# Token and weight sums of a two-level fast product moved and recut in a hybrid decoder step

## The chip, the cores and the metric

The kernel runs on one core of one Trainium2 chip. The core has TensorE (PE, matmuls; PEld is its weight load), VectorE (DVE), ScalarE (ACT), GpSimd (POOL) and SyncE (SP), which here issues nearly all DMAs. The metric is the device time of one execution in microseconds (us). Less is better.

## The reference

One step of a single-layer decoder for a prompt of 1024 tokens and 8 sample tokens (1032 columns in all), model width 2048. Everything is in float32.

```python
p = project(rmsnorm(x, norm_w), w_in)       # one product, 2048 x 7768, split by columns
att = dsa(p)        # indexer scores, top 256 keys, softmax attention, 8 heads x 128
h_ml = mlstm(p)     # 4 heads, chunked gated recurrence, states C, n, m
a  = att * silu(p['az'])
hn = h_ml * rsqrt(mean(h_ml ** 2) + 1e-6) * ml_norm_w
mo = hn * sigmoid(p['mo']) * silu(p['mz'])
y  = rmsnorm(x + concat([a, mo]) @ w_out, final_norm_w)
# also returned: k, v, indexer keys and the mLSTM states, of prompt and samples
```

The kernel keeps float32 accuracy by splitting each operand into a high part H (rounded for TensorE) and a low part L = x - H, and by adding three matmuls: HH, HL and LH.

## The kernel before, in words

**The projection.** The weights' columns are cut into 61 tiles of 128. Tile 0 is misc (indexer key, gates), tiles 1 to 8 the indexer's queries (iq), 9 to 16 the mLSTM values (computed by `vproj` with weights and tokens in both roles), 17 to 36 attention k, v, q and mLSTM q, k (`T_AK` = 17, `T_AQ` = 21, `T_MQ` = 29, `T_G` = 37), and 37 to 60 the 24 gate tiles. `proj` computes tiles 0 to 8 and 17 to 36 in four quarters each: a quarter loads 256 KB of weights, casts them (ACT makes H, DVE makes L) and multiplies. The tokens stay in SBUF, split, as `xH[k]` and `xL[k]`, k from 0 to 15. `evac` multiplies results by the row factors and writes them out through DMAs.

**The gate tiles** are computed in pairs by a seven-product scheme of the Strassen kind: tokens are cut into two halves of `HR` = 516 columns, k into two halves of 8, output columns into the two tiles of a pair (`NP` = 12 pairs). It needs four weight sums for each pair (`job_usum`, in DRAM as `usD`) and five token sums for each k of 8 (`job_prep`, in DRAM as `xsD`), both made beforehand, beside the projection. Then `gate_stage` runs 7 x 12 products of 48 matmuls of 258 columns (`CS`), `product`, each in two quarters q of the k range and two column pieces c. Products 4 and 6 (plain weights) come first, then 1, 3, 2 and at last 0 and 7. Partial results go out to `spD` (`put`) and come back (`get`); `combine` adds PSUM to them; `gate_mo`, `gate_mz` and `gate_az` apply tanh, the products with earlier results, and write `gateS`. `fill` brings token sums from `xsD` into the slots of `xH`, `xL` that are no longer wanted; the upper columns of `xH[8..15]`, `xL[8..15]` serve as buffers for split weights, and the `rstd` tile, the rings `wst` and `evp` lend spill buffers (`outs`).

**Jobs beside the main line.** Three lanes of generators are stepped after each quarter of a tile. A job has a start tile, an end tile and a weight, and is paced so that it ends at its end tile: lane 0 has the chunk gates, the indexer (`job_index`, DVE and ACT loops that find the top 256), the prompt's attention (`job_att`) and mLSTM (`job_ml`); lane 1 the token sums (`prep`, tiles 4 to 17), then the sample tokens' work (`dscore`, `dsel`, `datt`, `dml`); lane 2 the weight sums (`usum`, tiles 4 to 31). Their matmuls are ordered on PE between those of the tiles. The tool that builds the program orders each engine's instructions by its own timeline; what `pin` marks stays behind everything written before it on its engine.

`job_prep` works in 32 steps of one k and a quarter of the columns (`cw` = 129): two loads of `X`, three multiplications on DVE, four sums on POOL, one cast (L1375) and one subtraction (L1376) of all five sums, and two DMAs (L1378) to `xsD` with runs of 129 numbers. `sH` and `sL` have one buffer each. `job_usum` does, for each pair and each of four sums, a copy DRAM to DRAM issued by SP (L1387) and an accumulating DMA issued by POOL (L1389).

**PSUM.** Eight banks: three `pj` for the main products, five in the ring `bank()` for everything else. The gate stage takes a fourth for itself out of the ring for its whole length, so that two products alternate between two pairs of banks; the jobs have four.

After the gate stage, the output product `w_out` is computed, first for the last 264 columns, then for 768 columns by a seven-product scheme again, with the final norm.

Of the kernel before, what the change touches and what calls it, by code (L numbers as in the profile page):

```python
# [59 lines left out]
NX = 4  # L60
# [42 lines left out]
class Job:  # L103
    def __init__(self, name, start, end, weight, gen, *conds):
        self.name, self.start, self.end, self.weight, self.gen, self.conds = name, start, end, weight, gen, conds

# [43 lines left out]
def body(tc, A, stop=None):  # L150
# [8 lines left out]
    wst = ctx.enter_context(tc.tile_pool(name="wst", bufs=3))  # L159
# [52 lines left out]
    spD = dt_([3, NP, 2, 128, CS], "spD")  # L212
# [29 lines left out]
    evp = evctx.enter_context(tc.tile_pool(name="evp", bufs=6))  # L242
    xctx = ExitStack()
    xp = xctx.enter_context(tc.tile_pool(name="xp", bufs=1))
    xH = [xp.tile([128, R], F32R, name=f"xH{k}") for k in range(KT)]
    xL = [xp.tile([128, R], F32R, name=f"xL{k}") for k in range(KT)]
# [297 lines left out]
    def job_att():  # L544
# [4 lines left out]
        with tc.tile_pool(name="at", bufs=2) as pa:  # L549
# [65 lines left out]
            def soft(pair, S2):  # L615
                g, i, hp = pair
                cs = cuts((i + 1) * 128)
                for hh in range(2):
                    st = S2["st"][hh]
                    if len(cs) == 2:  # L620
                        V.tensor_tensor(st[:, 0:1], st[:, 0:1], st[:, 1:2], OP.max)
                    V.tensor_scalar(st[:, 2:3], st[:, 0:1], -ATT_SCALE, None, OP.mult)
# [4 lines left out]
                    if len(cs) == 2:  # L627
                        V.tensor_tensor(st[:, 3:4], st[:, 3:4], st[:, 4:5], OP.add)

            def start():  # L630
                return {"st": [pa.tile([128, 6], F32, name="st", bufs=4) for _ in range(2)], "P": [[], []]}
# [44 lines left out]
            for n, pair in enumerate(pairs):  # L676
# [21 lines left out]
                for hh in range(2):  # L698
                    V.reciprocal(cur["rc"][:, hp * 2 + hh, i:i + 1], now["st"][hh][:, 3:4])
# [82 lines left out]
    def job_ml():  # L782
        gT = mlc["gT"]
        with tc.tile_pool(name="ml", bufs=2) as pm:
# [72 lines left out]
            def main(c, h0, dk, dv, kv):  # L857
# [29 lines left out]
                for hh in range(2):  # L887
                    hms.append(pm.tile([128, 256], F32, name="hm"))
                    V.tensor_scalar(hms[hh], nds[hh][:, :256], st[:, 5, hh:hh + 1], None, OP.mult)
# [455 lines left out]
    def job_prep():  # L1345
        cw = CS // 2
        with tc.tile_pool(name="sx", bufs=1, side="right") as px:
            halves = rstd.rearrange("p (h t) -> p h t", h=2)
            steps = [(k, c) for k in range(8) for c in range(0, HR, cw)]

            def load(k, c):
                X = px.tile([128, 4, cw], F32, name="X", bufs=2)
                for y in range(2):
                    pin(SY.dma_start(X[:, 2 * y:2 * y + 2],
                                     A["xT"][k + 8 * y].rearrange("p (h t) -> p h t", h=2)[:, :, c:c + cw]))
                return X

            nxt = load(*steps[0])
            yield 1
            for n, (k, c) in enumerate(steps):  # L1360
                X = nxt
                if n + 1 < len(steps):
                    nxt = load(*steps[n + 1])
                O = px.tile([128, 5, cw], F32, name="O")
                lo, hi = nw[:, k:k + 1], nw[:, k + 8:k + 9]
                pin(V.scalar_tensor_tensor(X[:, 0:2], X[:, 0:2], lo, halves[:, :, c:c + cw], OP.mult, OP.mult))
                V.scalar_tensor_tensor(O[:, 0], X[:, 3], hi, halves[:, 1, c:c + cw], OP.mult, OP.mult)
                V.scalar_tensor_tensor(X[:, 2], X[:, 2], hi, halves[:, 0, c:c + cw], OP.mult, OP.mult)
                G.tensor_tensor(O[:, 1], X[:, 1], O[:, 0], OP.subtract)
                G.tensor_tensor(O[:, 2], O[:, 1], X[:, 0], OP.subtract)  # L1370
                G.tensor_tensor(O[:, 3], X[:, 0], X[:, 1], OP.subtract)
                G.tensor_tensor(O[:, 4], X[:, 2], O[:, 2], OP.add)
                yield 1
                H, L = (px.tile([128, 5, cw], F32R, name="s" + y) for y in "HL")
                pin(SC.copy(H, O))  # L1375
                V.tensor_tensor(L, O, H.bitcast(F32), OP.subtract)  # L1376
                for y, x in enumerate((H, L)):
                    SY.dma_start(xsD[:, k, y, :, c:c + cw].rearrange("o p t -> p o t"), x.bitcast(F32))  # L1378
                yield 1

# [20 lines left out]
    def ix_weight(blocks):  # L1401
# [10 lines left out]
             Lane([Job("prep", 4, T_AK, 65, job_prep),  # L1412
# [4 lines left out]
             Lane([Job("usum", 4, T_MQ + 2, 8 * NP, job_usum)])]  # L1417
# [189 lines left out]
    def gate_stage():  # L1607
        nonlocal pb0
        spare = [[x[8 + k][:, HR:HR + 512].rearrange("p (a b) -> p a b", a=4) for k in range(8)] for x in (xH, xL)]
        Hs, Ls = spare  # L1610
        free = [wst.tile([128, 4, 128], F32, name="w" + y, bufs=b)
                for y, b in (("raw", 2), ("H", 3), ("L", 3)) for _ in range(b)]
        raws, outs = free[:NX], [w.rearrange("p a b -> p (a b)") for w in free[NX:]]
        outs += [evp.tile([128, CN], F32, name="ev") for _ in range(6)]
        outs = [e[:, :CS] for e in outs]
        turn = {"raw": 0, "w": 0, "ev": 0}
        pj = [psj.tile([128, 512], F32, name=f"pj{x}") for x in range(3)] + [bank()]
        pj = [p[:, :CS] for p in pj]
# [630 lines left out]
```

## Time and profile before

| | us |
|---|---|
| median of 3 runs | 2232.45 (2230.85 to 2240.81) |
| the profiled execution | 2224.26 |
| its span, first to last instruction | 2222.5 |
| PE busy | 1982.8 |
| DVE, ACT, POOL busy | 1439.8, 943.1, 449.4 |
| mean granted TensorE clock | 0.95 |
| DMA | 440.96 MB in 340364 packets, mean 198 GB/s |

Busy time counts instructions that compute, not waits. A wait is listed as "who waited <- who ended the wait", with its total, count and longest. L and a number is a line of the kernel. A group's row has its count, busy us and mean ns, then the idle time of the engine just before its instructions and what ended it. Matmuls overlap in the pipeline, so their mean durations are longer than the time from one to the next.

### The profile page before, as it was taken

Reading aid. Unit: us, or ns where it says so; the run is one execution under the profiler, and the core shown is the slowest. Engines: PE = TensorE matmul, PEld = TensorE weight load, DVE = VectorE, ACT = ScalarE, POOL = GpSimd, SP = SyncE. Lnnn points to the kernel's source line nnn. Section 1 sums busy time; section 2 is a strip of 40 time slices with the busy share of each in tenths; the row PEclk is TensorE's granted clock in tenths of the full one; section 3 lists DMA queues with packets and bytes.
Section 4 is the critical chain, followed back from the end, with each engine's and each line's share of the span. In section 5 each row is a group of like instructions: output and inputs, shape, how many; then the busy total and the mean of one; then the engine's idle time right before and its main releaser. Section 6 shows DMA issues by size and latency. Waiting matters only on the chain. (4 is left out here: it accounts for less than half of the span.)

```text
span 2222.5 us, 37235 instructions
## 1 busy us (share of the span) xinstructions
PE 1982.8 (89%) x12710; PEld 1861.7 (84%) x12710; DVE 1439.8 (65%) x3451; ACT 943.1 (42%) x2025; POOL 449.4 (20%) x580
## 2 busy tenths in 40 slices
PE   9957368787899999999999999999988884999997
PEld 9956257676799999999999999999988884987886
DVE  8322325555566876869685555655577884789787
ACT  7111123343235323453133445446555553445555
POOL 0121211212223000100131000000355451104543
PEclk9988689988899999999999999999999997999999
DMA  6699999999767545532686665855788985888875
GB/s 233 142 181 158 181 193 212 185 194 178 175 186 208 163 132 148 132 82 69 200 251 179 203 197 154 244 166 171 208 260 258 278 252 155 293 300 285 290 254 185
DMA packets 340364, 440.96 MB, mean 198 GB/s; under 512 B 45430, under 2 KB 228534, under 8 KB 336334
## 3 DMA queue, kind: packets, MB, share of 16 engines
q1 hardware_dynamic: 330941, 399.06, 64.8%
q0 software_dynamic: 7936, 37.76, 8.6%
q8 instruction: 100, 1.64, 0.3%
q10 hardware_dynamic: 1296, 1.77, 0.2%
q14 instruction: 91, 0.74, 0.1%
HBM read 342.74 MB, written 146.05 MB: 220 GB/s over the span
## 5 line engine op out<-in xcount | busy, mean ns | idle before, releaser
L1464 PE MATMUL pj<-xH,wH 128*128 128x344 f32 (+1 forms) x1200 | 392.8, 330 | 44.6 <-DVE iqe L352 33.5
L1464 PE MATMUL pj<-xH,wL 128*128 128x344 f32 (+1 forms) x1200 | 393.1, 328 | 3.3 <-DVE wL L229 3.3
L1464 PE MATMUL pj<-xL,wH 128*128 128x344 f32 (+1 forms) x1200 | 393.3, 328 | 0.2 <-DVE xL L284 0.2
L1682 PE MATMUL pj<-xH,xL 128*128 128x258 f32 x1008 | 288.7, 286 | 1.2 <-DVE xL L1677 1.2
L1682 PE MATMUL pj<-xL,xH 128*128 128x258 f32 x1008 | 288.6, 286 | 0.0
L1682 PE MATMUL pj<-xH,xH 128*128 128x258 f32 x972 | 279.1, 287 | 4.4 <-DVE wH L1750 4.2
L1464 PEld LDWEIGHTS pj<-xH,wH 128*128 128x128 f32 x1200 | 229.8, 192 | 49.0 <-DVE iqe L352 34.8
L1464 PEld LDWEIGHTS pj<-xH,wL 128*128 128x128 f32 x1200 | 230.0, 192 | 5.2 <-DVE wL L229 4.3
L1464 PEld LDWEIGHTS pj<-xL,wH 128*128 128x128 f32 x1200 | 229.9, 192 | 1.4 <-DVE xL L284 0.7
L228 ACT CAST wH<-wraw 128x512 fp32r<-128x512 f32 (+2 forms) x183 | 109.7, 610 | 217.7 <-PE pj L1464 142.7
L1682 PEld LDWEIGHTS pj<-xH,xL 128*128 128x128 f32 x1008 | 192.8, 191 | 3.0 <-DVE xL L1677 1.4
L1682 PEld LDWEIGHTS pj<-xL,xH 128*128 128x128 f32 x1008 | 192.9, 191 | 1.0 <-issue 0.4
L1682 PEld LDWEIGHTS pj<-xH,xH 128*128 128x128 f32 x972 | 186.0, 191 | 6.0 <-ACT xH L1676 2.3
L229 DVE TENSOR_TENSOR wL<-wraw,wH 128x512 fp32r<-128x512 f32 (+2 forms) x183 | 127.0, 704 | 74.5 <-ACT wH L228 72.9
L513 ACT ACTIVATE eq<-eq 128x512 bf16<-128x512 bf16 (+2 forms) x93 | 78.4, 843 | 152.4 <-DVE eq L512 151.3
L1940 PE MATMUL pj<-wH,sH 128*128 128x512 f32 x336 | 132.4, 394 | 1.2 <-DVE yt L2054 0.8
L1940 PE MATMUL pj<-wH,sL 128*128 128x512 f32 x336 | 131.9, 393 | 0.0
L466 ACT ACTIVATE rl<-bank 128x512 f32<-128x512 f32 (+2 forms) x160 | 79.9, 523 | 118.4 <-PE bank L464 75.7
L1940 PE MATMUL pj<-wL,sH 128*128 128x512 f32 x336 | 126.2, 394 | 4.1 <-DVE wL L1929 4.0
L1376 DVE TENSOR_TENSOR sL<-O,sH 128x645 fp32r<-128x645 f32 x32 | 26.6, 830 | 133.5 <-DMA xsD<-sL 78.3
L469 DVE SCALAR_TENSOR_TENSOR s<-rl,wiN,s 128x512 f32<-128x512 f32 (+2 forms) x150 | 95.9, 661 | 23.6 <-ACT rl L466 22.1
L464 PE MATMUL bank<-ki,qi 128*128 128x512 f32 (+2 forms) x320 | 81.4, 368 | 20.8 <-DMA qi<-qS 14.2
(548 smaller groups left out, 5072.6 us busy)
## 6 DMA issues: line engine op xcount, KB each, us to landing
wraw<-in_wa_dram SPq DMA_DIRECT2D x146, 256.0 KB
wraw<-in_wt_dram SPq DMA_DIRECT2D x144, 256.0 KB
usD<-in_wa_dram POOLq DMA_DIRECT2D x48, 512.0 KB, 8.2
wraw<-in_wo_dram SPq DMA_DIRECT2D x64, 256.0 KB
usD<-in_wa_dram SPq DMA_DIRECT2D x24, 512.0 KB
usD<-usD SPq DMA_DIRECT2D x24, 512.0 KB
wraw<-usD SPq DMA_DIRECT2D x48, 256.0 KB
wH<-usD SPq DMA_DIRECT2D x48, 256.0 KB
```

Source lines behind the costliest of these rows:

```text
L228: a = SC.copy(H[:, s, :cols], raw[:, s, :cols])
L229: return a, V.tensor_tensor(L[:, s, :cols], raw[:, s, :cols], H[:, s, :cols].bitcast(F32), OP.subtract)
L464: PE.matmul(p[:, :cn], qi[:, h % 4, :], ki[x][:, c0:c0 + cn], start=(x == 0), stop=(x == 1))
L466: SC.activation(r[:, :cn], p[:, :cn], AF.Relu)
L469: v = V.scalar_tensor_tensor(s[:, c0:c0 + cn], r[:, :cn], wv, s[:, c0:c0 + cn], OP.mult, OP.add)
L513: SC.activation(junk2[:, :W1], junk2[:, :W1], AF.Copy, accum_out=cnt[:, 1:2])
L1376: V.tensor_tensor(L, O, H.bitcast(F32), OP.subtract)
L1464: m = PE.matmul(ps[:cols, :cn], w_[:, k, :cols], x_[kk][:, c0:c0 + cn], start=(kk == 0 and z == 0), stop=(kk == 15 and z == 2))
L1682: PE.matmul(ps[c], w_[:, k, :], x[y][:, c * CS:c * CS + CS], start=(first and q == 0 and k == 0 and z == 0), stop=(q == 1 and k == 3 and z ...
L1940: PE.matmul(ps[b], S_[x][:, b * 128:b * 128 + 128], T_[y], start=(k == 0 and z == 0), stop=(k == 7 and z == 2))
```

## The change

- **Token sums.** `job_prep` takes a whole k at a time: `X` [128, 2, 2, 516] is loaded by two DMAs with rows of 4128 B; two multiplications of 1032 numbers on DVE; four sums of 516 on POOL, in place but for `s1`; then, for each of the five sums, a cast and a subtraction of 516 numbers into one tile `hl` [128, 2, 516] (one buffer) and one DMA to `xsD` with rows of 2064 B. `X`, `s1` and `hl` have one buffer each. The job yields 56 times where it did 65.
- **Weight sums.** `usum` runs from tile 11 to 36.5 where it ran from 4 to 31, and is finished before the gate stage.
- **Rings.** `wst` and `evp` become one big tile for each name, cut into slots (class `Ring`), and `xH`, `xL` one tile each for all k, so that wider pieces can be taken out of them.
- **Gate stage, weights.** A product loads, casts and subtracts its weights at once (1024 numbers a partition, 512 KB) where it did two halves; three raw buffers, four split pairs.
- **Gate stage, spills.** One tile of 516 columns for both pieces c of a product: one `put`, one `get`, one tanh pair. The second operand of `gate_mz` and `gate_az` still comes in two pieces of 258, into two buffers `ones`.
- **Banks.** The fourth bank is taken only for products 4 and 6 and for 0 and 7; products 1, 3 and 2, now each in a loop of its own, rotate over the three `pj` banks (`two`).
- **Small operations.** In the attention, maximum, scaling, sum and reciprocal of two heads are done by one DVE operation each; in the mLSTM the scaled `hm` is made by ACT instead of DVE.

```diff
+class Ring:
+    def open(self):
+        for name, (n, width, dt) in self.tags.items():
+            self.big[name] = self.pool.tile([128, n, width], dt, name=name, bufs=1)
+            self.turn[name] = 0
+    def tile(self, shape, dt, name, bufs=None):
+        i = self.turn[name] % n
+        x = self.big[name][:, i]
...
-    wst = ctx.enter_context(tc.tile_pool(name="wst", bufs=3))
+    wst = Ring(ctx.enter_context(tc.tile_pool(name="wst", bufs=1)),
+               {"wraw": (2, 512, F32), "wH": (3, 512, F32R), "wL": (3, 512, F32R)})
...
-    spD = dt_([3, NP, 2, 128, CS], "spD")
+    spD = dt_([3, NP, 128, HR], "spD")
...
+    XH, XL = (xp.tile([128, KT, R], F32R, name="x" + y) for y in "HL")
+    xH = [XH[:, k] for k in range(KT)]
...
     def soft(pair, S2):
+                if len(cs) == 2:
+                    V.tensor_tensor(sv[:, :, 0], sv[:, :, 0], sv[:, :, 1], OP.max)
+                V.tensor_scalar(sv[:, :, 2], sv[:, :, 0], -ATT_SCALE, None, OP.mult)
...
-                    V.tensor_scalar(hms[hh], nds[hh][:, :256], st[:, 5, hh:hh + 1], None, OP.mult)
+                    SC.activation(hms[hh], nds[hh][:, :256], AF.Copy, scale=st[:, 5, hh:hh + 1])
...
     def job_prep():
-            steps = [(k, c) for k in range(8) for c in range(0, HR, cw)]
...
+            def load(k):
+                X = px.tile([128, 2, 2, HR], F32, name="X")
                 for y in range(2):
+                    pin(SY.dma_start(X[:, y].rearrange("p h t -> p (h t)"), A["xT"][k + 8 * y]))
                 return X
+            for k in range(8):
+                X = load(k)
                 yield 1
+                a11, a21, a12, a22 = (X[:, y, h] for y in range(2) for h in range(2))
+                for y in range(2):
+                    pin(V.scalar_tensor_tensor(X[:, y], X[:, y], nw[:, k + 8 * y:k + 8 * y + 1], halves, OP.mult, OP.mult))
+                s1 = px.tile([128, HR], F32, name="s1")
+                G.tensor_tensor(s1, a21, a22, OP.subtract)
+                G.tensor_tensor(a21, a11, a21, OP.subtract)
+                G.tensor_tensor(a11, s1, a11, OP.subtract)
+                G.tensor_tensor(a12, a12, a11, OP.add)
                 yield 1
+                for n, x in enumerate((a22, s1, a11, a21, a12)):
+                    hl = px.tile([128, 2, HR], F32R, name="hl")
+                    pin(SC.copy(hl[:, 0], x))
+                    V.tensor_tensor(hl[:, 1], x, hl[:, 0].bitcast(F32), OP.subtract)
+                    SY.dma_start(xsD[n, k].rearrange("z p t -> p z t"), hl.bitcast(F32))
+                    yield 1
...
-             Lane([Job("prep", 4, T_AK, 65, job_prep),
+             Lane([Job("prep", 4, T_AK, 56, job_prep),
-             Lane([Job("usum", 4, T_MQ + 2, 8 * NP, job_usum)])]
+             Lane([Job("usum", 11, T_G - 0.5, 8 * NP, job_usum)])]
...
     def gate_stage():
-        pj = [psj.tile([128, 512], F32, name=f"pj{x}") for x in range(3)] + [bank()]
+        halves = [[X[:, k:k + 2, HR:HR + 512] for k in range(8, 16, 2)] for X in (XH, XL)]
+        free = [wst.plain(name) for name in ("wraw", "wH", "wL")]
+        raws = [w[:, 0:2] for w in free]
+        ones = [w[:, 2, :CS] for w in free[1:]]
+        evs = evp.big["ev"].rearrange("p a b -> p (a b)")
+        outs = [evs[:, x * HR:x * HR + HR].rearrange("p (c t) -> p c t", c=2) for x in range(4)]
+        pj = [psj.tile([128, 512], F32, name=f"pj{x}")[:, :CS] for x in range(3)]
...
+        def product(kind, i, slot, ps, first=True):
+            with tc.high_priority():
+                raw = take("raw", raws)
+                SY.dma_start(raw, wget(kind, i))
+                H, L = (x[turn["w"] % 4] for x in halves)
+                SC.copy(H, raw)
+                V.tensor_tensor(L, raw, H.bitcast(F32), OP.subtract)
             for q in range(2):
...
+        extra = bank()[:, :CS]
+        both = (pj[:2], [pj[2], extra])
...
+        def two():
+            return [take("p", pj), take("p", pj)]
+        for i in range(NP):
+            e, ps = get(0, i), two()
+            product(1, i, 1, ps)
             with tc.high_priority():
+                put(1, i, combine(ps, e, OP.add))
...
+        both = (pj[:2], [pj[2], bank()[:, :CS]])
...
+    lanes[2].ensure("usum")
     gate_stage()
+    wst.open()
```

More of the change, by code (lines that the diff above doesn't have):

```diff
@@ L1651, in tick @@
             state["u"] += 1
[L1652 to L1654 removed]
+            if fills:
+                fills.pop(0)()
             if todo:
@@ L1706, in half_tanh, with gate_mo, gate_mz @@
             SC.activation(out, out, AF.Identity, bias=1.0)
-        def gate_mo(j, cs, e):
+        def gate_mo(j, h, e):
             half_tanh(e, e)
-            SY.dma_start(row(8 + j)[:, cs], e)
-        def gate_mz(j, cs, e):
-            g = ev()
-            SY.dma_start(g, row(8 + j)[:, cs])
+            SY.dma_start(row(8 + j)[:, cut(h)], flat(e))
+        def gate_mz(j, h, e):
+            gs = [take("one", ones) for _ in range(2)]
             s2 = ev()
             half_tanh(s2, e)
-            G.tensor_tensor(e, g, e, OP.mult)
+            for c in range(2):
+                SY.dma_start(gs[c], row(8 + j)[:, cut(h)][:, c * CS:c * CS + CS])
+                G.tensor_tensor(e[:, c], gs[c], e[:, c], OP.mult)
@@ L1718, in gate_mz, with gate_az @@
             G.tensor_tensor(s2, s2, e, OP.mult)
-            SY.dma_start(row(8 + j)[:, cs], s2)
-        def gate_az(j, cs, e):
-            n = min(CS, S - cs.start)
-            g = ev()
-            SY.dma_start(g[:, :n], rcS[j // 4][j % 4, cs.start:cs.start + n].partition_broadcast(128))
+            SY.dma_start(row(8 + j)[:, cut(h)], flat(s2))
+        def gate_az(j, h, e):
+            gs = [take("one", ones) for _ in range(2)]
             s2 = ev()
             half_tanh(s2, e)
-            G.tensor_tensor(e[:, :n], g[:, :n], e[:, :n], OP.mult)
+            for c in range(2):
+                t0 = h * HR + c * CS
+                n = min(CS, S - t0)
+                SY.dma_start(gs[c][:, :n], rcS[j // 4][j % 4, t0:t0 + n].partition_broadcast(128))
+                G.tensor_tensor(e[:, c, :n], gs[c][:, :n], e[:, c, :n], OP.mult)
@@ L1747, in combine, with gate @@
-        def combine(ps, es, op, outs_=None):
-            res = outs_ or es
-            for c in range(2):
-                V.tensor_tensor(res[c], ps[c], es[c], op)
-            return res
-        late = []
+            SY.dma_start(flat(e), row(j)[:, cut(0)])
+            gate_az(j, 0, e)
+        def gate(i, x, h, e):
+            if i < NM:
+                (gate_mo, gate_mz)[x](i, h, e)
+            elif x == 0 and h == 0:
+                SY.dma_start(row(2 * (i - NM))[:, cut(0)], flat(e))
+                late.append(2 * (i - NM))
+            else:
+                gate_az(2 * (i - NM) + x, h, e)
```

187 lines of the change are left out of this document (65 added, 122 removed).

## The prediction

> **What bounds the kernel now.** I read the page first, then the busy time by stages, then the waits of the one bad stage. The span, the busy line of TensorE and the three rows of slices:
>
> ```profile
> span 2222.5 us, 37235 instructions
> PE 1982.8 (89%) x12710; PEld 1861.7 (84%) x12710; DVE 1439.8 (65%) x3451; ACT 943.1 (42%) x2025; POOL 449.4 (20%) x580
> PE   9957368787899999999999999999988884999997
> PEclk9988689988899999999999999999999997999999
> DMA  6699999999767545532686665855788985888875
> ```
>
> TensorE (PE) carries the time, but 240 us of the span it is idle, and the idle slices are not spread: they stand in slices 3 to 11 and 30 to 34. In the first group the DMA row is all nines and the granted clock falls; in the second neither is so plain. The busy time by stages, cut where the trace shows tiles and stages begin (columns: stretch, length, busy us of PE, PEld, DVE, ACT, POOL, granted clock, DMA share, GB/s):
>
> ```profile
> 84.40:101.50 17.10, 17.10 (x100) 17.10 (x99) 5.22 (x13) 3.31 (x6) 0.60 (x2) 1.00 0.61 149
> 101.50:214.90 113.40, 76.62 (x385) 74.33 (x384) 33.98 (x64) 17.42 (x30) 23.69 (x40) 0.83 0.98 176
> 214.90:541.50 326.60, 224.92 (x949) 188.68 (x947) 148.40 (x386) 108.23 (x238) 59.85 (x107) 0.84 1.01 189
> 541.50:628.50 87.00, 72.64 (x425) 70.48 (x425) 49.81 (x110) 24.52 (x56) 21.18 (x27) 0.89 0.74 183
> 628.50:1101.00 472.50, 472.29 (x3030) 461.98 (x3029) 349.91 (x908) 179.04 (x347) 55.81 (x67) 1.00 0.51 140
> 1101.00:1619.00 518.00, 510.19 (x4101) 498.82 (x4101) 323.15 (x861) 247.89 (x580) 51.18 (x62) 1.00 0.68 200
> 1619.00:1826.00 207.00, 179.18 (x1407) 173.76 (x1406) 166.35 (x515) 118.35 (x311) 104.89 (x161) 0.97 0.90 267
> 1826.00:1900.00 74.00, 43.22 (x274) 39.57 (x273) 40.43 (x98) 27.10 (x64) 14.18 (x17) 0.77 0.60 172
> 1900.00:2222.00 322.00, 304.43 (x1579) 257.92 (x1578) 262.67 (x415) 167.45 (x330) 113.21 (x86) 0.99 0.79 269
> ```
>
> The rows are tile 4; tiles 5 to 8; the v stage (tiles 9 to 16); tiles 17 and 18; tiles 19 to 36; the gate stage in two parts; the change to the output product; the output. Tiles 5 to 8 take 28 us each where tile 4, with the same 96 matmuls, takes 17.1 us at full clock. What TensorE and its helpers wait for in the 440 us from 101.5 to 541.5:
>
> ```profile
> ACT sH L1375 <- DMA xsD<-sH: 146.2, 20, 13.0
> DVE sL L1376 <- DMA xsD<-sL: 78.3, 13, 14.4
> ACT wH L1528 <- DMA wraw<-in_wv_dram: 42.6, 18, 6.4
> PE bank L1533 <- ACT wH L1528: 41.6, 13, 6.9
> PE pj L1464 <- DVE iqe L352: 33.5, 4, 12.4
> PE pj L1533 <- DVE iqe L352: 29.3, 1, 29.3
> ```
>
> Two roads lead from the DMA engines to TensorE: weights land late (third and fourth row), and ScalarE and VectorE stand in their own order behind the single pair sH, sL of the token sums (first two rows), so that evacuations come late (last two). This is the stage that the change rewrites.
>
> **The floor of that stage.** Tile 4's row gives 17.1 us for 96 x 388 columns, 0.459 ns a column at full clock. Tiles 5 to 8: 4 x 17.1 = 68 us. The v stage by its loops: 240 matmuls of 512 columns, 240 of 480 and 384 of 392, 388,608 columns, and the indexer's:
>
> ```profile
> L464 PE MATMUL bank<-ki,qi x76: 280/340/767, 336.0 to 541.1; 128*128 128x384 f32 x38, 128*128 128x512 f32 x32, 128*128 128x256 f32 x6
> ```
>
> 32,512 more; together 421,120 x 0.459 = 193 us. Floor 262 us of the 440.
>
> **What the DMA engines carry there.** First the queues' rows of 101.5 to 541.5 (packets, MB, share of 16 engines) with the accumulates issued in it, then the same row of 1900 to 2000, where most packets are weights of 2 KB:
>
> ```profile
> q1 hardware_dynamic: 81745, 70.21, 84.3%
> q0 software_dynamic: 1695, 11.13, 15.5%
> usD<-in_wa_dram POOLq DMA_DIRECT2D x22, 512.0 KB, 10.0
> ```
>
> ```profile
> q1 hardware_dynamic: 16309, 29.99, 88.4%
> ```
>
> The engines are full (99.8% of 440 us). On q1 a packet of 859 B takes 0.843 x 440 x 16 / 81745 = 73 ns; at the end one of 1839 B takes 0.884 x 100 x 16 / 16309 = 87 ns: twice the bytes for a fifth more time. Now the token sums, from the issues of the whole page and from the groups of the stage (x29 of 32 steps lie in it):
>
> ```profile
> xsD<-sH SPq DMA_DIRECT2D x32, 322.5 KB
> xsD<-sL SPq DMA_DIRECT2D x32, 322.5 KB
> X<-in_xT_dram SPq DMA_DIRECT2D x64, 129.0 KB
> ```
>
> ```profile
> L1376 DVE TENSOR_TENSOR sL<-O,sH 128x645 fp32r<-128x645 f32 x29 | 24.1, 831 | 133.5 <-DMA xsD<-sL 78.3 <-ACT wH L228 24.6 <-ACT sH L1375 22.4
> L1375 ACT CAST sH<-O 128x645 fp32r<-128x645 f32 x29 | 21.1, 728 | 146.2 <-DMA xsD<-sH 146.2
> L1366 DVE SCALAR_TENSOR_TENSOR X<-X,nw,rstd 128x258 f32<-128x258 f32 x28 | 13.7, 490 | 18.3 <-DMA X<-in_xT_dram 18.1
> L1368 DVE SCALAR_TENSOR_TENSOR X<-X,nw,rstd 128x129 f32<-128x129 f32 x31 | 11.2, 362 | 33.8 <-DMA X<-in_xT_dram 33.8
> ```
>
> They move 29.6 MB in pieces of 129 numbers (516 B): 57,344 packets, 52,000 of them here. At 73 ns each that is 236 us of all 16 engines; counted by bytes alone (26.8 of 70.21 MB of q1's 371 us) 142 us. After the change the same bytes are 10,240 packets of 2064 B and 2,048 of 4128 B; by the 87 ns for 1839 B, scaled by bytes, 97 and 195 ns, 87 us. **Saved: 55 to 149 us** of DMA time. The weight sums: 22 accumulates on q0 (68 us) and 22 base copies of 512 KB on q1 (by bytes 61 us). Begun at tile 11 instead of 4 and spread to 36.5, 48 x 6/25.5 = 11 of them fall into tiles 11 to 16, so **63 us leave the stage**. DMA need: 440 - 63 - (55 to 149) = 228 to 322 us.
>
> **The stage's new time.** Neither need nor floor alone sets it. With the middle of the need (275) in some 300 us the share is 0.9; the row nearest to that is 1619 to 1826 (share 0.90, PE busy 179 of 207 us, 87%). 262 / 0.87 = 303 us: **gain 137 us**, bounds 178 (floor) and 0 (the chain, below). Engines there: VectorE's work on the token sums goes from 32 x (0.831 + 0.490 + 2 x 0.362) = 65 us to 16 x 1.28 + 40 x 0.72 = 49 us (1032 numbers extrapolated from the last two rows, 516 from the row of 512 below); ScalarE stays at 24 us (40 x 0.62 for 32 x 0.73); SP issues 56 DMAs where it issued 128. GpSimd's 128 short sums become 32 of 516 numbers, 1.6 us each by the row of 512 below. What is queued behind: each of the 40 casts waits for the landing of the last piece (one buffer hl, where sH and sL were two single ones), and stands on ScalarE before weight casts; the piece's DMA stands on SP before weight loads. Weights are cast up to two quarters ahead (8 us), which covers a few us of such a wait and not ten.
>
> **Tiles 17, 18:** end of the sums' spill, 87 us with PE busy 72.6 at clock 0.89, so 65 of work. I take half of the 22: **10 us** (0 to 22). **Tiles 19 to 36:** PE idle 0.2 of 472 us beside a DMA share of 0.51. One accumulate per 705/48 = 14.7 us (estimate: six tiles of the v stage at 230 us for eight, 77 for two, some 455 to tile 36.5) instead of
>
> ```profile
> L1389 POOL DMA_DIRECT2D usD<-in_wa_dram x48: 756/781/1187, 107.6 to 941.6; - x48
> ```
>
> one per 17.4 adds some 60 us of DMA to a stage with 230 us free: **0** (0 to -10). If that cover were gone, the 63 us would come back here.
>
> **The gate stage.** The rows that price its parts, from groups by form, and two waits of TensorE in it:
>
> ```profile
> L1676 ACT CAST xH<-wraw 128x512 fp32r<-128x512 f32 x82 | 50.5, 617 | 65.4 <-PE pj L1682 43.9 <-DMA wraw<-in_wa_dram 20.4 <-DMA gateS<-wH 0.6
> L1677 DVE TENSOR_TENSOR xL<-wraw,xH 128x512 fp32r<-128x512 f32 x82 | 59.3, 723 | 31.4 <-ACT xH L1676 29.9 <-PE pj L1682 0.3
> L1967 POOL TENSOR_TENSOR yt<-yt,fnr 128x512 f32<-128x512 f32 x18 | 28.4, 1599 | 35.6 <-ACT jk L1960 35.6
> L889 DVE TENSOR_SCALAR hm<-bank,st 128x256 f32<-128x256 f32 x32 | 14.0, 478 | 5.5 <-POOL st L885 5.2
> L622 DVE TENSOR_SCALAR st<-st 128x1 f32<-128x1 f32 x64 | 8.9, 149 | 0.1
> ```
>
> ```profile
> PE bank L897 <- DVE hm L889: 10.2, 8, 3.6
> PE pj L1682 <- DVE wH L1750: 4.2, 2, 2.2
> ```
>
> Wide splits: 645 numbers cost ScalarE 111 ns and VectorE 108 ns more than 512, so 1024 cost 1.05 and 1.14 us; 84 wide for 168 narrow save 16 and 25 us. Merged small ops: 96 fewer at 0.15 us, 14 us of VectorE. hm moves 15 us from VectorE to ScalarE. All this lies beside TensorE, which is idle 8 us in 518 before 1619: worth nothing there. After 1619 there are 28 us idle, after 1826 31 us. There hm's wait (10.2 us) may go; ScalarE then waits for GpSimd in VectorE's place, with weight casts behind it. The fifth bank is with the other jobs only in the middle three of five kinds of product, while three banks serve the products: the next product's second half may start 24 matmuls (24 x 258 x 0.459 ns = 2.8 us) after the half that used the bank ended, where it had a whole product more. One spill tile per product: half the DMAs, 2064 B instead of 1032. I take **+10 us**, from -20 (late combines, half a us in each of 36 products) to +45 (most of the 59 idle gone). **The output** is unchanged but for views: 0.
>
> **The sum.** 137 + 10 + 0 + 10 = 157 us. 2222.5 - 157 = 2065.5; the profiled run took 2224.26 in all, 1.8 more, and the median of the three runs, 2232.45, stands 8.2 above that. Against the median: 2232.45 - 157 = **2075 us**.
>
> **A rule against it.** The Trainium skill, DMA: Bandwidth & Descriptors, section Specifications, puts the smallest transfer for line rate at 512 B; by it 516 B pieces have nothing to gain, which would be the first rival below. The trace speaks against it: 73 ns for 859 B, 87 ns for 1839 B.
>
> **Rivals.** (1) The pieces' length changes nothing and only the 63 us of weight sums leave: the stage takes 377 us, gain 63 + 10 + 10, time 2150. For it: q1's mean is of mixed packets in a full queue, so 73 ns may be waiting and not work. Against: the two rows above.
> (2) The single buffer is the chain: each piece costs 0.62 + 0.72 + 0.6 us of issue and a landing of 146.2/20 = 7.3 us as sH waited, 40 x 9.2, and each k some 16 us more (load, two scalings, four sums of 1.6): 498 us, as long as now. The stage stays; 20 us of gain elsewhere: 2212. Against: that landing was measured behind full engines. By the fixed 2 us and 436 GB/s of the same page's section Anatomy of one DMA — SWDGE (gpsimd) path, a 528 KB piece would land in 3.2 us and the chain be 40 x 5.1 + 128 = 333 us; no row here shows a piece landing alone.
> (3) Slower: in the gate stage a product's one wide split no longer runs ahead (its slots lie across two k of one big tile, beside token slots that matmuls still read; were the whole stretch taken as one, a split would wait for the product before). Then 1.05 + 1.14 us stand before each of 84 products: 184 us, time 2259. It decides from 1.9 us a product on. Against: now its matmuls' longest wait, the 4.2 us of the row above, is for a combine (L1750) and not for a split, and the rings keep three raw and four split pairs.
>
> **Chances.** Forecast (2035 to 2115) 0.57; better (stage at its floor, gate stage at its best: down to 1987) 0.10; rival 1 (2115 to 2190) 0.20; rival 2 0.07, half of it within what a measurement of this kernel can tell (about 0.5%, 11 us); rival 3 0.06. Range 2025 to 2170.
>
> **What would show it.** Tiles 5 to 8 near 17 to 20 us each, the v stage near 230, clock back at 1.0, DMA share below 0.95; casts of hl waiting 2 to 4 us, not 7. Wrong if hl's casts wait as sH did, if the DMA row keeps its nines to tile 17, or if matmuls of the gate stage wait for splits or for combines.

## The result, and the profile after

| | before | after |
|---|---|---|
| median | 2232.26 us (2230.85 to 2240.81) | 2101.68 us (2095.27 to 2103.95, 4 runs) |
| profiled execution, its span | 2224.26, 2222.5 us | 2095.27, 2093.5 us |
| mean granted clock | 0.95 | 0.97 |

The ratio is 0.9403, 95% interval [0.9372, 0.9434]: 131 us less (predicted: 157 less, 2075 us). The page of the changed kernel, its span, busy line and slices:

```profile
span 2093.5 us, 35967 instructions
PE 1952.4 (93%) x12710; PEld 1844.0 (88%) x12710; DVE 1416.4 (68%) x3167; ACT 926.3 (44%) x1885; POOL 417.1 (20%) x452
PE   9999979879998999998899999999969987999997
PEclk9999989989999999999899999999989998999999
DMA  7466877867766453638853848538989887898875
```

The hole in the PE row (slices 3 to 11 before) is gone, and the DMA row has no run of nines there any more. By stages, the cuts at the same tiles as before (tile 4; tiles 5 to 8; v stage; tiles 17 and 18; tiles 19 to 36; gate stage in two parts; change to the output product; its first part), columns as in the prediction:

```profile
85.60:102.70 17.10, 17.10 (x100) 17.09 (x99) 6.10 (x12) 3.31 (x6) 1.12 (x2) 1.00 0.62 160
102.70:175.40 72.70, 70.00 (x386) 69.34 (x385) 29.09 (x44) 17.64 (x32) 8.74 (x8) 0.98 0.59 175
175.40:408.90 233.50, 203.31 (x944) 174.16 (x942) 151.17 (x323) 104.80 (x236) 43.66 (x38) 0.96 0.77 230
408.90:496.40 87.50, 69.97 (x424) 68.85 (x425) 52.75 (x121) 26.50 (x62) 19.52 (x22) 0.86 0.72 199
496.40:983.70 487.30, 477.00 (x3034) 466.13 (x3032) 349.91 (x910) 180.21 (x348) 64.16 (x78) 0.99 0.58 155
983.70:1730.50 746.80, 699.07 (x5569) 681.57 (x5567) 486.76 (x1229) 361.67 (x777) 152.43 (x200) 0.97 0.72 225
1730.50:1741.70 11.20, 0.29 (x4) 0.09 (x2) 2.21 (x7) 3.92 (x8) 5.24 (x6) 0.63 0.61 202
1741.70:1840.00 98.30, 96.71 (x768) 96.29 (x769) 68.01 (x108) 44.84 (x88) 11.95 (x14) 0.97 0.82 264
```

The same stages of the kernel before that the prediction cut elsewhere (tiles 20 to 36; whole gate stage; from its last matmul to the first of the output product; first part of the output):

```profile
668.60:1101.00 432.40, 432.19 (x2755) 422.85 (x2754) 324.27 (x867) 166.19 (x319) 44.27 (x55) 1.00 0.50 136
1101.00:1826.30 725.30, 689.67 (x5507) 672.88 (x5507) 489.80 (x1375) 366.54 (x893) 156.37 (x222) 0.99 0.74 219
1826.30:1865.40 39.10, 12.11 (x64) 10.43 (x62) 17.47 (x51) 11.48 (x31) 12.26 (x15) 0.65 0.40 103
1865.40:1969.20 103.80, 99.66 (x768) 97.27 (x769) 74.28 (x127) 48.40 (x97) 11.54 (x14) 0.97 0.84 268
```

The balance of the two profiled executions, span against span (129.0 us):

| stage | before | after | gain | predicted |
|---|---|---|---|---|
| up to tile 5 | 101.5 | 102.7 | -1.2 | 0 |
| tiles 5 to 16 | 440.0 | 306.2 | +133.8 | +137 |
| tiles 17, 18 | 87.0 | 87.5 | -0.5 | +10 |
| tiles 19 to 36 | 472.5 | 487.3 | -14.8 | 0 |
| gate stage and change to the output | 764.4 | 758.0 | +6.4 | +10 |
| output | 357.1 | 351.8 | +5.3 | 0 |

One term made nearly all of the gain and came out near its forecast; tiles 17 and 18 gave nothing, tiles 19 to 36 lost 15 us, and the gate stage gave less than was taken. In tiles 5 to 16 of the changed kernel, these are the waits, the q1 queue, and the groups of the new token sums:

```profile
ACT hl L1395 <- DMA xsD<-hl: 67.2, 23, 7.3
DVE hl L1396 <- ACT hl L1395: 56.0, 23, 5.2
ACT wH L1547 <- DMA wraw<-in_wv_dram: 25.2, 10, 4.7
PE bank L1552 <- ACT wH L1547: 6.1, 5, 1.9
```

```profile
q1 hardware_dynamic: 37347, 61.38, 63.0%
```

```profile
L1396 DVE TENSOR_TENSOR hl<-X,hl 128x516 fp32r<-128x516 f32 x28 | 24.2, 865 | 49.6 <-ACT hl L1395 49.4
L1386 DVE SCALAR_TENSOR_TENSOR X<-X,nw,rstd 128x1032 f32<-128x1032 f32 x14 | 18.0, 1290 | 18.6 <-DMA X<-in_xT_dram 18.6
L1395 ACT CAST hl<-X 128x516 fp32r<-128x516 f32 x28 | 17.4, 621 | 66.9 <-DMA xsD<-hl 52.9 <-DVE X L1386 9.5 <-issue 4.2
```

q1 has 37,347 packets where it had 81,745, and is busy 0.630 x 306.2 = 193 us where it was 0.843 x 440 = 371. ScalarE still waits for the landing of the piece before, 2.9 us each time that it waits (67.2 / 23) and 67 us in all, but TensorE's own waits for a weight cast (L1533 before, L1552 now) fell from 41.6 to 6.1 us.

### The profile page after: what moved, and what is told of

Read it like the earlier page. It is cut to its first block, busy times and chain, and to the rows that moved or that the text cites. A ratio compares the mean times of both kernels' runs of the same rounds, so it can differ in the third digit from the quotient of the medians.

```text
span 2093.5 us, 35967 instructions
## 1 busy us (share of the span) xinstructions
PE 1952.4 (93%) x12710; PEld 1844.0 (88%) x12710; DVE 1416.4 (68%) x3167; ACT 926.3 (44%) x1885; POOL 417.1 (20%) x452
## 5 line engine op out<-in xcount | busy, mean ns | idle before, releaser
L1698 PE MATMUL pj<-xH 128*128 128x258 f32 x1152 | 331.7, 288 | 27.3 <-ACT xH L1690 13.1
L1698 PE MATMUL pj<-xL,xH 128*128 128x258 f32 x1152 | 330.8, 287 | 0.0
L1698 PE MATMUL pj<-xH,xL 128*128 128x258 f32 x1152 | 330.2, 287 | 0.0
L1698 PEld LDWEIGHTS pj<-xH 128*128 128x128 f32 x1152 | 220.2, 191 | 31.6 <-ACT xH L1690 13.8
L1698 PEld LDWEIGHTS pj<-xL,xH 128*128 128x128 f32 x1152 | 220.4, 191 | 1.5 <-issue 0.8
L1698 PEld LDWEIGHTS pj<-xH,xL 128*128 128x128 f32 x1152 | 220.3, 191 | 1.0 <-issue 0.4
L1895 PE MATMUL bank<-mH,wH 128*128 128x264 f32 x256 | 74.3, 291 | 12.5 <-ACT wH L251 12.5
```

Of the source, the lines that this page charges most:

```text
L1698: PE.matmul(ps[c], w_[:, q, ks], x[y][:, c * CS:c * CS + CS], start=(first and q == 0 and k == 0 and z == 0), stop=(q == 1 and k == 3 and ...
L1895: PE.matmul(p, w_[:, k, :], x_, start=(n == 0), stop=(n == 47))
```

## The experiments

All times are medians against the kernel before on the same chip; stage figures come from one profile of each kernel.

| kernel | token sums | weight sums | gate stage, banks, small operations | us | ratio to before |
|---|---|---|---|---|---|
| b_usum | old | tiles 11 to 36.5 | old | 2185.36 | 0.9819 [0.9788, 0.9851] |
| b_prep | new | tiles 4 to 31 | old | 2124.62 | 0.9555 [0.9524, 0.9585] |
| c_gate | old | tiles 4 to 31 | new | 2197.93 | 0.9893 [0.9872, 0.9915] |
| a_oldprep | old | tiles 11 to 36.5 | new | 2165.62 | 0.9734 [0.9704, 0.9765] |
| a_usum4 | new | tiles 4 to 31 | new | 2093.44 | 0.9421 [0.9378, 0.9464] |
| c_same (the change) | new | tiles 11 to 36.5 | new | 2098.61 | 0.9431 [0.9407, 0.9455] |

**The parts alone.** Weight sums moved, in the kernel before:

```diff
-             Lane([Job("usum", 4, T_MQ + 2, 8 * NP, job_usum)])]
+             Lane([Job("usum", 11, T_G - 0.5, 8 * NP, job_usum)])]
...
+    lanes[2].ensure("usum")
     gate_stage()
```

> The kernel before with one part of the change alone: weight sums from tile 11 to 36.5 instead of 4 to 31. Theory (DMA time is the limit from tile 5 to 16; long pieces and the later weight sums each take their share out): 63 of the stage's 440 us of DMA work leave, stage near 377 us, time near 2170; tiles 19 to 36 lengthen from 472 towards 487 us if the weight sums are what lengthened them. Rival (length of pieces is nothing, the weight sums are all): stage near 306 us, time near 2100. Rival (the token sums' own waits are all): stage stays at 440, time 2232 to 2247.

The new `job_prep` (as in the change) in the kernel before:

```diff
-            steps = [(k, c) for k in range(8) for c in range(0, HR, cw)]
+            for k in range(8):
+                X = load(k)
...
-             Lane([Job("prep", 4, T_AK, 65, job_prep),
+             Lane([Job("prep", 4, T_AK, 56, job_prep),
```

> The kernel before with one part of the change alone: token sums per whole k in rows of 2064 B. Theory: DMA need of tiles 5 to 16 falls by 55 to 149 us, middle 102, so the stage takes near 340 us and the time is near 2135. Rival (length of pieces is nothing): stage near 440, time near 2232. Rival (the token sums are all, the weight sums cost nothing there): stage near 306 us, time near 2100.

Tiles 5 to 16 and then tiles 20 to 36 of the first, and of the second:

```profile
102.60:487.60 385.00, 297.68 (x1328) 260.44 (x1327) 183.06 (x451) 125.60 (x267) 75.66 (x136) 0.88 0.94 179
614.30:1053.60 439.30, 434.19 (x2755) 424.64 (x2754) 324.58 (x867) 166.52 (x319) 51.18 (x64) 0.99 0.59 156
```

```profile
103.10:422.20 319.10, 278.74 (x1327) 244.11 (x1326) 180.37 (x362) 122.98 (x265) 57.73 (x55) 0.97 0.82 239
554.60:987.70 433.10, 432.03 (x2753) 422.79 (x2753) 323.45 (x867) 166.66 (x319) 43.68 (x55) 1.00 0.50 136
```

Alone, the move takes 55 us off the stage and gives 7 back in tiles 20 to 36; the new token sums take 121 us off and give nothing back there. 55 + 121 is 176, and the change with both got 134: the two do not add up. The time falls by less than the stage, by 37 us in b_usum and 97 in b_prep, mainly because the gate stage is 12 and 14 us longer than before (737.4 and 739.3 us for 725.3). Against what was expected: b_usum's stage is 8 us longer than its first theory said and the gain smaller (37 us, not 62); b_prep's stage is 21 us shorter, and its time is as forecast.

**The parts taken out of the change.**

```diff
-             Lane([Job("usum", 11, T_G - 0.5, 8 * NP, job_usum)])]
+             Lane([Job("usum", 4, T_MQ + 2, 8 * NP, job_usum)])]
```

> The changed kernel with the weight sums back at tiles 4 to 31. Theory: the stage of tiles 5 to 16 grows from 306 to near 340 us, tiles 19 to 36 fall from 487 to near 472 us, time near 2120. Rival (weight sums cost nothing in that stage): stage stays near 306, tiles 19 to 36 near 472, time near 2087, better than the change. Rival (weight sums are all): stage near 440, time near 2220.

The other one has the old `job_prep` and its 65 yields in the changed kernel.

> The changed kernel with the old token sums (quarter columns, rows of 516 B). Theory: stage near 377 us instead of 306, time near 2172. Rival (length of pieces is nothing): time near 2102. Rival (token sums are all of it): stage near 440, time near 2235.

a_oldprep came out near its first theory (stage 386 us, ratio 0.9734); a_usum4 did not: its stage of 315 us is nearer to the rival's 306 than to the theory's 340. The same two stretches, of a_usum4 and of a_oldprep, then tiles 20 to 36 of the change itself:

```profile
104.30:419.50 315.20, 279.55 (x1328) 245.19 (x1327) 178.92 (x362) 122.86 (x265) 57.21 (x55) 0.96 0.83 242
549.50:983.00 433.50, 432.02 (x2753) 422.78 (x2753) 323.52 (x866) 166.44 (x318) 43.60 (x55) 1.00 0.50 137
```

```profile
101.10:487.00 385.90, 299.08 (x1328) 259.98 (x1326) 182.64 (x450) 125.66 (x267) 75.92 (x136) 0.88 0.94 179
615.30:1056.90 441.60, 434.19 (x2754) 424.45 (x2753) 323.92 (x866) 166.44 (x318) 51.03 (x64) 0.99 0.58 156
```

```profile
537.20:983.70 446.50, 436.20 (x2755) 426.38 (x2753) 322.52 (x866) 166.43 (x318) 51.64 (x64) 0.99 0.57 152
```

With the long token sums the DMA engines have room (share 0.83 with the weight sums in the stage, 0.73 without), and moving the weight sums saves 9 us of the stage (315.2 to 306.2). It gives back 13 in tiles 20 to 36 (433.5 to 446.5, where PE is idle 10.3 us and not 1.5). The time is the same within the intervals: beside the long token sums, moving the weight sums gained nothing. With the weight sums late, tiles 20 to 36 took 439 to 448 us in all profiles, with them early 432 to 434 (before, b_prep, a_usum4, c_gate and c_best). The prediction had put 0 there, with 10 as the worst.

**The length of the rows alone.** The spill of the token sums in rows of 516 B, all else as in the change:

```diff
-    xsD = dt_([5, 8, 2, 128, HR], "xsD")
+    xsD = dt_([5, 8, 2, 4, 128, HR // 4], "xsD")
...
-                    SY.dma_start(xsD[n, k].rearrange("z p t -> p z t"), hl.bitcast(F32))
+                    for z in range(2):
+                        SY.dma_start(xsD[n, k, z].rearrange("c p t -> p c t"),
+                                     hl[:, z].bitcast(F32).rearrange("p (c t) -> p c t", c=4))
```

> The changed kernel with the same operations and buffers for the token sums, but the spill of each piece cut into rows of 516 B again (two DMAs a piece, four runs a row), which the gate stage reads back in rows of 516 B too. Theory (what a packet costs, not what it holds): 30,720 more packets at some 73 ns on 16 engines, 125 us more DMA work on top of 223, so the stage of tiles 5 to 16 goes from 306 to some 350 to 385 us; time 2145 to 2185. Rival (the new order of operations and its fewer waits are the gain): stage stays near 306 to 320, time near 2105 to 2120.

Measured: 2153.56 us, ratio 0.9678 [0.9641, 0.9716], some 55 us over the change (0.9431 for c_same, below). Its stage, queue and wait:

```profile
102.60:462.50 359.90, 294.22 (x1328) 255.07 (x1326) 188.90 (x384) 125.01 (x274) 55.89 (x48) 0.91 0.77 190
```

```profile
q1 hardware_dynamic: 66348, 62.81, 67.3%
```

```profile
ACT hl L1395 <- DMA xsD<-hl: 112.6, 27, 8.4
```

29,001 more packets for nearly the same bytes cost q1 0.673 x 359.9 - 193 = 49 us of 16 engines, 27 ns a packet, and the stage 54 us. The stage and the time lie where the theory put them, but partly by luck: the added work is 49 us and not 125. So rival 1 of the prediction falls: the length of the rows counts by itself, on engines that are not full. The DMA share is just 0.77: what grew is the cast's wait for the landing, 4.2 us each (112.6 / 27) for 2.9, 45 us in all. So the rows seem to act here through the single buffer; short rows with two buffers were not run. That the number of DMAs (two for each piece here) is not the reason is made likely by c_inplace below, which also has two and is faster. Reading the same rows back is cheaper: in the gate stage 27,057 more packets cost q1 0.703 x 757.0 - 0.690 x 746.8 = 17 us, 10 ns a packet, and the gate stage is 10 us longer.

**How much the single buffer costs.**

```diff
-                    hl = px.tile([128, 2, HR], F32R, name="hl")
-                    pin(SC.copy(hl[:, 0], x))
-                    V.tensor_tensor(hl[:, 1], x, hl[:, 0].bitcast(F32), OP.subtract)
-                    SY.dma_start(xsD[n, k].rearrange("z p t -> p z t"), hl.bitcast(F32))
+                    h = px.tile([128, HR], F32R, name="hl", bufs=2)
+                    pin(SC.copy(h, x))
+                    V.tensor_tensor(x, x, h.bitcast(F32), OP.subtract)
+                    SY.dma_start(xsD[n, k, 0], h.bitcast(F32))
+                    SY.dma_start(xsD[n, k, 1], x)
```

> The changed kernel itself, so that the three others have it on the same chip. Ratio to before 0.940, as measured; stage from tile 5 to tile 17 306 us.

> The changed kernel, but a token sum's piece no longer has both halves in one buffer hl: the half H goes into one of two buffers by turns, the half L is written over the sum itself, and each is stored by a DMA of its own with the same rows of 2064 B. A cast then no longer waits for the landing of the piece just before it. What is tested: how much of the 44 us that the stage still stands above TensorE's 262 us (306 measured) is the single buffer hl. My theory: the 67 us that ScalarE waited there were partly on the path; most of these waits go, the stage takes 285 to 300 us, the time falls by 5 to 20 us (ratio to before 0.931 to 0.938). The rival: the waits are covered by casts made ahead, the stage stays at 303 to 309 us and the time within 5 us (ratio 0.938 to 0.943). A second rival: 80 landings instead of 40 and sums that hold X longer make it worse, over 312 us.

Measured: 2074.46 us, ratio 0.9335 [0.931, 0.9359], against 0.9431 [0.9407, 0.9455] for c_same on the same chip: 24 us less (5 to 20 expected; the ratio lies in the expected range), and the fastest version of all. The stage of c_same and of c_inplace, then the wait of each:

```profile
102.70:408.60 305.90, 272.78 (x1328) 242.46 (x1326) 179.33 (x366) 123.00 (x268) 52.34 (x46) 0.97 0.74 218
101.60:395.60 294.00, 272.13 (x1328) 245.09 (x1326) 186.55 (x383) 125.78 (x272) 58.38 (x49) 0.97 0.78 231
```

```profile
ACT hl L1395 <- DMA xsD<-hl: 71.6, 23, 7.3
ACT hl L1395 <- DMA xsD<-hl: 21.6, 7, 6.8
```

The wait fell from 71.6 us to 21.6, and the stage from 305.9 to 294.0. Tiles 17 to 19 gave 9 us more (130.7 to 121.8), which this run's expectation had not counted; the last piece is cast at 410 us instead of 440. Thus part of rival 2 of the prediction was true: without the chain through `hl` the change is 24 us faster.

> As the kernel before it, and the weight sums begun at tile 4 again as in the kernel before the change. If the weight sums' DMA work costs nothing in the stage once the token sums are long and the cast does not wait, this is the same as the kernel before it within 5 us, ahead of the changed kernel by what that one gains. If the later weight sums are worth something, it is 5 to 15 us slower than the kernel before it.

Measured: 2102.61 us, ratio 0.9466 [0.9439, 0.9493], 28 us slower than c_inplace; neither of the two expected sizes. Its tiles 5 to 16 and tiles 20 to 36, and its waits for weights:

```profile
103.90:442.00 338.10, 285.82 (x1331) 249.87 (x1329) 188.41 (x386) 126.96 (x276) 63.12 (x60) 0.93 0.84 237
564.30:996.70 432.40, 432.05 (x2754) 422.80 (x2754) 323.79 (x865) 166.62 (x318) 43.61 (x55) 1.00 0.50 137
```

```profile
ACT wH L1548 <- DMA wraw<-in_wv_dram: 53.3, 20, 9.9
```

Here moving the weight sums is worth 44 us of the stage, where with the single buffer it was worth 9. Put the other way, with the weight sums early the two buffers gain nothing: the stage is 23 us longer than in a_usum4, and the ratio (0.9466, for 0.9421 there) is not told apart. The share is the same as in a_usum4 (0.84 and 0.83), yet weights land later: this wait was 27.8 us there. One reading is that the single buffer also paced the token sums, so that they did not pile up against the weight loads; no run separates that, and it stays open.

**The gate stage and what goes with it.** c_gate is the change with the old token sums and the old place of the weight sums.

> The changed kernel with both the old token sums (pieces of 516 B) and the old place of the weight sums (tiles 4 to 31.5): what is left of the change are the wide splits, the spill tile per product, the fifth bank and the merged small operations. My theory: by the gate stage and the change to the output product, 6 us together, and the 5 us of the output, 0.985 to 0.998 of the time before. The rival, that the first is the gain of the mLSTM's end alone and the other parts cost: 0.998 to 1.005. Stage from tile 5 to tile 17 as before the change, 435 to 445 us.

Measured: 23 us less than before (ratio 0.9893), in the range of the theory, but the gate stage gives more of it than 6 us. Its gate stage, the change to the output product and the output's first part:

```profile
1098.10:1833.60 735.50, 697.47 (x5568) 681.43 (x5567) 485.03 (x1228) 362.16 (x777) 155.57 (x198) 0.98 0.71 223
1833.60:1843.70 10.10, 0.25 (x3) 0.04 (x1) 2.01 (x7) 3.73 (x8) 5.24 (x6) 0.70 0.63 203
1843.70:1940.00 96.30, 96.24 (x767) 95.82 (x768) 66.15 (x106) 44.92 (x88) 11.89 (x14) 0.98 0.82 268
```

The first two rows make 745.6 us for 764.4 before: 19 us of gain, and the output 7.5 more. In the change the same two make 758.0. The other runs show where the difference comes from. With the old gate code (gate stage, banks and small operations as before) the gate stage grew from 725.3 us to 737.4 in b_usum and 739.3 in b_prep; with the new code from 735.5 in c_gate to 746.0 in a_oldprep, 749.2 in a_usum4 and 746.8 in the change. So changing the token sums or the weight sums lengthens the gate stage by 10 to 14 us, with either code. The new code itself is worth nearly the same in three pairs, gate stage and change to the output taken together: 19 us (before and c_gate), 17 (b_prep and a_usum4) and 18 (b_usum and a_oldprep). Why the stage lengthens, no run shows; with the old code TensorE is busy 697.2 us in b_usum and 699.3 in b_prep, for 689.7 before, with nearly the same number of matmuls (x5508 and x5507), and the granted clock is 0.98 and 0.97 for 0.99.

Three of the waits of PE in the gate stage of the change:

```profile
PE pj L1698 <- ACT xH L1690: 13.1, 1, 13.1
PE pj L1698 <- DVE rstd L1768: 11.2, 6, 5.3
PE bank L923 <- ACT hm L915: 7.8, 4, 3.7
```

The first is one wait near the stage's start (a wide split whose weights came late); in c_gate the same wait is 5.8 us. The first 12 products took 90 us (983.7 to 1073.8) in the change and 82 in c_gate; in the change and in c_same the last two accumulates of the weight sums are issued only there (993.6 and 1011.4 us in the change), after the stage has begun: `ensure` puts them ahead of it in the program, not in time. The 13 us also stand in c_same and c_inplace, and 6 in a_usum4, c_best, c_gate, but 6 in a_oldprep too, whose weight sums are late as well: the late sums alone do not explain it, and as a_oldprep's gate stage is no shorter than the others, this wait does not explain the 10 to 14 us either.

Three single parts of it were taken back in the changed kernel. The split in two halves again:

```diff
-                SY.dma_start(raw, wget(kind, i))
-                SC.copy(H, raw)
-                V.tensor_tensor(L, raw, H.bitcast(F32), OP.subtract)
+                with tc.high_priority():
+                    SY.dma_start(raw[:, q], wget(kind, i)[:, q])
+                    SC.copy(H[:, q], raw[:, q])
+                    V.tensor_tensor(L[:, q], raw[:, q], H[:, q].bitcast(F32), OP.subtract)
```

> The changed kernel with the weights of a product loaded, cast and subtracted in two halves again, in the same buffers. Theory (the wide piece costs the gap of 13 us at the third product, where TensorE waits for a wide cast whose load landed late, and nothing else): gate stage from 747 to near 735 us, time 8 to 13 us shorter. Rival (the load is late whatever its width, since it is issued late): gap and time as they are. Rival (wide splits save work that matters): gate stage longer by up to 20 us.

Measured: ratio 0.9469 [0.9442, 0.9495]; not told apart from the change, where 8 to 13 us less were expected. The longest wait for a split is 8.6 us, not 13.1, but the gate stage is 753.9 us long, 7 more than in the change (746.8), not 12 less: the theory fell, and the second rival, that wide splits save work that matters, fits better.

`hm` on VectorE again (a `tensor_scalar` in place of the activation at L915):

> The changed kernel with the scaling of hm back on VectorE. Theory (the bank, not hm, is what moved the mLSTM forward): time within 5 us, the mLSTM still ends before the last product. Rival (hm on ScalarE moved it): the mLSTM ends 20 us or more later and the time grows by 10 to 25 us.

Measured: ratio 0.9437 [0.9405, 0.9468], the same, as the theory said; TensorE's wait for hm is 17.3 us and not 7.8, and nothing of it shows in the time.

The fourth bank held through the whole stage again, so that the jobs have four banks as before:

```diff
-        del extra, both
         def two():
-            return [take("p", pj), take("p", pj)]
+            return take("p", both)
...
-        both = (pj[:2], [pj[2], bank()[:, :CS]])
```

> The changed kernel with the fourth bank of the products kept out of the ring for the whole gate stage, products alternating between two pairs of banks throughout. Theory (the fifth bank lets attention and mLSTM run earlier, so that the mLSTM ends before the last product): the last mLSTM transposes move from 50 us before the end of the products to after it, the way from the last product to the first output matmul grows from 11 to near 39 us, and the matmuls' 11 us of waits for combines go: time 10 to 25 us longer. Rival (the bank does nothing, the mLSTM was sped up by moving hm to ScalarE): order and time as they are or 11 us shorter.

Measured: 2115.20 us, ratio 0.9514 [0.9486, 0.9542], slower than the change by about 18 us (0.9431 for c_same), as expected. Its gate stage, the change to the output product and the output's first part:

```profile
983.10:1717.40 734.30, 695.44 (x5543) 678.48 (x5541) 477.06 (x1197) 352.88 (x755) 157.82 (x199) 0.98 0.69 222
1717.40:1752.20 34.80, 4.23 (x30) 3.38 (x28) 7.49 (x17) 8.93 (x19) 4.62 (x8) 0.62 0.70 138
1752.20:1859.70 107.50, 99.97 (x767) 97.82 (x768) 73.66 (x130) 48.57 (x98) 12.16 (x14) 0.96 0.81 260
```

The gate stage itself is 12 us shorter with four banks of its own (some 4 of them go with jobs' matmuls that now come later: PE busy 695.4 for 699.1), but the mLSTM, short of a bank, ends after the last product (its last transposes at 1734 us, against 1678 and 52 us before the last product in the change), and 24 us are lost in the change to the output and 9 in the output. Of the three parts taken back, only the fifth bank for the jobs shows a gain in the time.

## Why the prediction was right, and where its terms were off

**The stage, 137 predicted, 134 measured.** The step that short rows are DMA work held: the stage took 306.2 us for 303 predicted, tiles 5 to 8 18.2 us each (72.7 / 4), the v stage 233.5, the DMA share 0.59 and 0.77, the casts' waits 2.9 us. The pieces cost what they were priced at but for one: 1.29 us a scaling (1.28 was taken; its two rows give 1.26) and 0.62 a cast, 0.87 a subtraction where 0.72 was taken. The clock came back to 0.98 and 0.96, not to 1.0. But nearly all of the gain is the token sums' (125 us in a_usum4, 121 in b_prep); the weight sums, taken at 63 us of DMA work, brought 9 of it. And two sizes on the way were off, in opposite directions, so that the 3 us between 137 and 134 are partly luck.

The first is the DMA need, put at 228 to 322 us; share times length is 0.73 x 306.2 = 224 us, just below. The token sums saved q1 0.858 x 385.9 - 193 = 138 us with the weight sums late (81,593 packets at 85.8% in a_oldprep), and 0.843 x 440 - 0.634 x 319.1 = 169 us in the kernel before (38,171 packets at 63.4% in b_prep): near the top of the 55 to 149, and over it. (The 87 us of the long rows are those of all 32 steps, the 236 and 142 of the short ones those of 29, which makes the forecast saving some 8 us too low.) Of the 138, 49 are the rows of the spill (a_short). The other 89 go with the loads of `X` in short rows and with a fuller queue, which no run separated.

The second is the share of 0.9, by whose row the 87% was taken. TensorE was busy 89% of the stage (273.3 of 306.2 us), but beside a DMA share of 0.73. What held it there in part was the chain through `hl`: without it, in c_inplace, the stage is 12 us shorter with no DMA work taken away (q1 0.669 x 294.0 = 197 us). The prediction had this chain as rival 2, as an alternative to the forecast; it was a part of it. Its price of 9.2 us a piece was too high, since the 7.3 us in it were waited behind full engines, as was said against it; the wait is 2.9 us now. The Trainium skill, DMA: Bandwidth & Descriptors, section Anatomy of one DMA — SWDGE (gpsimd) path, by whose figures the landing was estimated at 3.2 us, has them for DMAs that GpSimd issues, and these are issued by SP. No trace shows how long a whole piece takes to land: a wait is only the part of a landing that ScalarE sees. The one landing on record, of half a piece (258 KB) in c_best, has a median of 4.6 us at a DMA share of 0.84.

**The weight sums.** That 63 us of DMA work leave the stage was right as work (0.94 x 385.0 = 362 us in b_usum for 440 before, 78 less), and worth 55 us there; it was wrong to add it to the token sums' saving as if DMA time still set the end. With the token sums long and the single buffer `hl` it saved 9 us of the stage, and tiles 20 to 36 gave 13 back; with two buffers it saved 44. What it is worth depends on what else the stage waits for. The step "beside a stage with 230 us free: 0" failed, and the loss went beyond the 10 us that it allowed: the accumulates' mean share was free there, and TensorE still went idle for 10 us at single places, each time for VectorE (6 us around the sample tokens' count L1050, and at the end of tile 36):

```profile
PE bank L1050 <- DVE cb L1048: 3.5, 2, 3.0
PE bank L966 <- DVE ot L1286: 3.5, 1, 3.5
```

How the later weight sums bring this about, no run shows.

**Tiles 17 and 18, 10 predicted, 0 measured.** The token sums' spill is not what TensorE's own waits name. Its longest waits of that stretch, two before and one after:

```profile
PE pj L1464 <- DVE ev L352: 5.6, 1, 5.6
PE pj L1464 <- DVE im L509: 4.3, 1, 4.3
```

```profile
PE bank L1014 <- issue: 13.7, 1, 13.7
```

Before, evacuations were late; after, it is the first matmul of the sample tokens' scores. "issue" names no cause, but in a_usum4 the trace does, for the same matmul:

```profile
L1014 PE MATMUL bank<-bd,kp 128*128 128x128 f32 x256 | 34.6, 285 | 10.6 <-DMA kp<-in_cik_dram,idx 7.5 <-DVE bd L1009 3.1
```

`kp` holds keys that GpSimd gathers by an indexed DMA. In the change the first gather is issued at 457.8 us, the matmul starts at 470.6, and the slowest gather took 12.5 us to land, so it is most likely the same wait. What the stretch gained, it lost again there.

**The gate stage, 10 predicted, 6.4 measured, 19 in c_gate.** The bounds held, but 6.4 is a sum of two things: 17 to 19 us for the new gate code, as the three pairs show, less the 10 to 14 by which the gate stage lengthens when the stage of tiles 5 to 16 is eased. The prediction had no term for the second. Rival 3, a wide split late before each of 84 products, did not come: one split was late, by 13 us. That TensorE waits for combines (11.2 us on the `rstd` buffer) came too, so that both of the prediction's signs against itself in this stage appeared, at a small size; a_4bank shows up to 12 us for the three banks, within the 20 that the prediction gave as the loss. The gain is that the jobs end before the last product, through the fifth bank (a_4bank). The output, predicted at 0, gained 5 us, all in its first part. VectorE has 108 instructions there and not 127 (the counts behind x in the rows), which fits with work of the jobs that had run over before.

**A rule against it.** The Trainium skill, DMA: Bandwidth & Descriptors, section Specifications, names 512 B as the smallest transfer for line rate. The measurement decides: writing rows of 516 B in place of 2064 B cost 27 ns for each added packet and 54 us of the stage.

## What to carry to other kernels

Two savings on one resource need not add up, since after the larger one something else may set the end: rework the floor and the next chain before the second is counted. Here one and the same move was worth 55, 9 or 44 us of its stage, by what else stood in it. A buffer that must land before the next cast makes the time of one small DMA, and so the length of its rows, count on the path even where the DMA engines have a quarter of their time free; two halves in buffers of their own got 24 us here with the weight sums late, and nothing with them early. Where side jobs and the main products share PSUM banks, look at which of them ends last: a bank that costs the products up to 12 us was worth more to the jobs. And measure a part in more than one setting: the new gate code looks worth 6 us in the balance and 17 to 19 in three pairs of runs.

## What was not expected of the hardware

Rows of 516 B cost more than their bytes when they are written: a row of 2064 B cut into four adds three packets of 27 ns, 81 ns (a_short, tiles 5 to 16), and three of 10 ns, 30 ns, in the gate stage, where the same rows are read back. With the 97 ns that the prediction estimated for 2064 B, a written packet of 516 B takes about (97 + 81) / 4 = 45 ns, an estimate from these rows.

A mean DMA share far from full goes with idle TensorE: in tiles 20 to 36 the profiles with the weight sums late have PE idle 5 to 12 us of some 445, at a share of 0.56 to 0.59, and those with them early 0 to 2 of 433, at 0.50. The late weight sums come with both, so the share is not shown to be the cause.
